# Late modulation in chunks that are loaded a step ahead and pinned on VectorE, head outputs loaded a group ahead, and half of the down weights in the activation buffers

## The chip, the cores and the metric

One core of one Trainium2 chip. The metric is the device time of one execution in microseconds (us); the lower the better. Matrix products run on TensorE (PE in the profile), elementwise work on VectorE (DVE) and ScalarE (ACT), and nearly all loads are issued in program order by SyncE (SP).

## The reference

One layer of a diffusion backbone: 512 latent tokens and 256 context tokens of width 2048. All matrix products are in fp32.

```python
mod = jax.nn.silu(c) @ w_mod[l] + b_mod[l]
sh1, sc1, ga1, sh2, sc2, ga2 = jnp.split(mod[:, None, :], N_MOD, axis=-1)
...
p_lat = modulate(rmsnorm(x, g_pre_mix[l]), sh1, sc1) @ w_in[l]
p_ctx = modulate(rmsnorm(ctx, g_pre_mix[l]), csh1, csc1) @ w_in[l]
m_lat, m_ctx = mlstm_group(p_lat, p_ctx, ...)      # 8 heads of 128
d_lat, d_ctx = diff_group(p_lat, p_ctx, cos, sin, lam, ...)   # 8 heads of 128
y_lat = jnp.concatenate([m_lat, d_lat], axis=-1).astype(x.dtype) @ w_out[l]
x = x + ga1 * rmsnorm(y_lat, g_post_mix[l])
h_lat = modulate(rmsnorm(x, g_pre_ffn[l]), sh2, sc2)
x = x + ga2 * rmsnorm(conv_ffn(h_lat, w_up[l], conv_ffn_w[l], conv_ffn_b[l], w_down[l]), g_post_ffn[l])
```

`sh1` and `sc1` are needed at once (`wmA`). The other four modulations (`ga1`, `sh2`, `sc2`, `ga2`, `wmB`, four times 2048 x 2048) are needed only after the heads: this is the late modulation.

## The kernel before

The kernel is one program in stages: start and first projections (0 to 240 us of the span), the head stage (240 to 1140), the first three groups of the output projection (1140 to 1262), its last group and the transition (1262 to 1380), the up projection (1380 to 2222), and the down projection with the end (2222 to 2733).

**Weights.** Every fp32 weight is split into two parts, `hi` (a cast on ScalarE) and `lo` (the rest, on VectorE), and each product is three matmuls: `whi` by `hi`, `whi` by `lo`, `wlo` by `hi` (`mm3`). A weight block arrives in raw tiles of 128 x 1024 (512 KB, pool `raw` with three buffers, shared with the late modulation), and `load_w` splits it into four `whi` and `wlo` tiles of 512 columns.

**Head stage.** `proj(m, with_ctx)` multiplies one weight block of 128 outputs with the latent tokens (`mm`, 512 columns) and, where asked, the context tokens (`cx`, 256 columns), in four groups g of four k tiles. For each head there are the projections diff_k, diff_v, mlstm_k and mlstm_v with context, and from head 5 on three latent projections (`lat_tile`). In this stage TensorE's instructions are pinned in program order, and `tick()` inserts pieces of the heads' attention between the matmuls: scores (`sc`), softmax (`mx` reduction on VectorE, `p` on ScalarE), transposes (`pt`), outputs. ScalarE's and VectorE's instructions are placed by the scheduler unless the code pins them.

**Late modulation.** It runs on VectorE. `modb_steps` is a generator: for each of 16 column blocks (q, cc) it loads raw tiles of `wmB` and adds them, scaled by the conditioning, into `macc` (L267 for the first, L269 for the others). A block is four steps of two raw tiles. `modb_cols` then sums over the partitions on TensorE (`modr`) and puts the columns into `mcol` (L283, L286). `step(limit)` runs one step: at the end of each projection and once at the start of heads 1 to 4 (limit 48, that is q = 0 to 2); the last 16 steps run in the down projection, at even `cc`.

**Output and down projection.** `nat_group` multiplies one group of four activation tiles (`mhi`, `mlo`) with four weight blocks and adds the products to `y` (L901). `get_mix(k)` brings a head output back, partly from DRAM (`mixr`). In the down projection odd `cc` take their weights through two wide tiles (`vhi`, `vlo`).

Of the kernel before, what the change touches and what calls it, by code (L numbers as in the profile page):

```python
# [6 lines left out]
F32 = mybir.dt.float32  # L7
F32R = mybir.dt.float32r
AF = mybir.ActivationFunctionType
ALU = mybir.AluOpType  # L10
# [4 lines left out]
P = 128  # L15
# [19 lines left out]
MIXG = [[0, 1, 2, 3], [8, 9, 10, 11], [4, 5, 12, 13], [6, 7, 14, 15]]  # L35
# [23 lines left out]
class Prog:  # L59
# [37 lines left out]
    def slot(self, name, dt=F32):  # L97
        return self.p_slot.tile([P, 512], dt, tag="slot", name=name)

    def load_w(self, src, n, act=False, wide=False):  # L100

        his, los = [], []
        if act:
            bh, bl = self.act("wact"), self.act("wact")
        if wide:
            for j in range(n // 1024):
                raw = self.p_raw.tile([P, 1024], F32, tag="raw", name="raw")
                self.nc.sync.dma_start(raw, src[:, j * 1024:(j + 1) * 1024])
                hi, lo = self.wide_w()
                self.split(hi, lo, raw)  # L110
                for q in range(2):
                    his.append(hi[:, q * 512:(q + 1) * 512])
                    los.append(lo[:, q * 512:(q + 1) * 512])
            n = 0
        for j in range(n // 512):
            if j % 2 == 0:
                w = min(1024, n - j * 512)
                raw = self.p_raw.tile([P, 1024], F32, tag="raw", name="raw")
                self.nc.sync.dma_start(raw[:, :w], src[:, j * 512:j * 512 + w])
            if act:  # L120
                hi, lo = bh[:, j, :], bl[:, j, :]
            else:
                hi = self.p_w.tile([P, 512], F32R, tag="whi", name="whi")
                lo = self.p_w.tile([P, 512], F32R, tag="wlo", name="wlo")
# [14 lines left out]
    def act(self, name):  # L139
        return self.p_act.tile([P, 4, 512], F32R, tag="act", name=name)  # L140

    def split(self, hi, lo, src):
        self.nc.scalar.copy(hi, src)  # L143
        self.nc.vector.tensor_tensor(lo, src, hi.bitcast(F32), ALU.subtract)  # L144

    def mm3(self, ps, whi, wlo, ahi, alo, start, stop, **k):
        mm = self.mm
# [103 lines left out]

    def modb_steps(self):

        nc, I = self.nc, self.I
        for q in range(4):
            for cc in range(4):
                acc = self.slot("macc")
                for kg in range(4):
                    for j in range(4):
                        if j % 2 == 0:  # L260
                            raw = self.p_raw.tile([P, 1024], F32, tag="raw", name="raw")
                            nc.sync.dma_start(raw, I["wmB"][q, cc, kg, :, j * 512:(j + 2) * 512])
                        kc = kg * 4 + j
                        c = self.c1[:, kc:kc + 1]
                        r = raw[:, j % 2 * 512:(j % 2 + 1) * 512]
                        if kc == 0:
                            nc.vector.tensor_scalar(acc, r, c, None, ALU.mult)  # L267
                        else:
                            nc.vector.scalar_tensor_tensor(acc, r, c, acc, ALU.mult, ALU.add)  # L269
                    if kg < 3:  # L270
                        yield
                self.defer(12, lambda q=q, cc=cc, acc=acc: self.modb_cols(q, cc, acc))
                yield

# [23 lines left out]
    def phase_in(self):  # L298
        nc, I = self.nc, self.I
        pc = self.p_c  # L300
        self.modc = pc.tile([P, KT, 4], F32, name="modc_sb")
        self.bA1 = pc.tile([P, KT], F32, name="bA1")
        self.c1 = pc.tile([P, KT], F32, name="c1")
        self.nlam = pc.tile([P, 1], F32, name="nlam")
        self.gg_d = self.dram.tile([2, D], F32, name="gg_d")
        self.mcol = pc.tile([P, 64], F32, name="mcol")

        lam = self.slot("lam")[:, :256]
        nc.sync.dma_start(lam, I["cols"][:, COLS["lam"][0]:])
# [12 lines left out]
        self.mix_d = self.dram.tile([KT, P, TL], F32, name="mix_d")  # L322
        self.acc_d = self.dram.tile([48, P, TL], F32, name="acc_d")
        self.acc = {}
        with self.tc.tile_pool(name="start", bufs=2) as self.p_st, \
                self.tc.tile_pool(name="mraw", bufs=4) as self.p_mr:
            self.startup()
            self.spill([b + h for h in (1, 2, 3) for b in (MQ, MO, DQ)])
            self.context()
            for base in (MQ, MO, DQ):  # L330
                self.lat_tile(base + 4)
            self.spill([b + 4 for b in (MQ, MO, DQ)])
        with self.tc.tile_pool(name="at1", bufs=1) as self.p_at1, \
                self.tc.tile_pool(name="cst", bufs=2) as self.p_cst, \
                self.tc.tile_pool(name="a3", bufs=14) as self.p_a3:
            self.attn_setup()
            self.pin = True
            self.gates_in(*self.proj(MG, True))
            self.queues[0].append(self.gates())
            for h in range(NH):  # L340
                if h >= 5:
                    for base in (MQ, MO, DQ):
                        self.lat_tile(base + h)
                elif h >= 1:
                    for base in (MQ, MO, DQ):
                        t = self.slot("accr")
                        nc.sync.dma_start(t, self.acc_d[base + h])
                        self.acc[base + h] = t
                hd = Head()
                if 0 < h < 5:  # L350
                    self.step(48)
                self.diff_q(hd, h)
                self.diff_k(hd, h, *self.proj(DK + h, True))
                self.diff_v(hd, h, *self.proj(DV + h, True))
                self.queues[1].append(self.diff_rest(hd, h))
                self.mlstm_qo(hd, h)
                self.mlstm_k(hd, h, *self.proj(MK + h, True))
# [95 lines left out]
    def proj(self, m, with_ctx):  # L453
        get = self.load_w(self.I["w1"][m], 2048)
# [4 lines left out]
        for g in range(4):  # L459
# [4 lines left out]
            if with_ctx:  # L464
                for kt in range(4 * g, 4 * g + 4):
                    c = self.chl[kt]
                    self.mm3(psc, *get(kt * P, P), c[:, :TC], c[:, TC:], kt == 0, kt == KT - 1)
                self.tick()
        self.step(48)
        return psl, psc  # L470


# [427 lines left out]
        else:  # L900
            nc.vector.tensor_tensor(y[tt][cc], ps, y[tt][cc], ALU.add)  # L901

    def nat_group(self, wsrc, acts, y, first, pool, tag, down=False):

        for cc in range(4):
            get = self.load_w(wsrc(cc), 2048, wide=down and cc % 2 == 1)
            if down and cc % 2 == 0:
                self.step(64)
            for tt in range(4):
                self.nat_unit(get, acts, tt, y, cc, first, pool, tag)  # L910

# [40 lines left out]
    def new_ss(self):  # L952
        return self.p_s.tile([P, 4], F32, tag="ss4", name="ss4", bufs=4)

    def mix_acts(self, g):
        hi, lo = self.act("mhi"), self.act("mlo")
        for j, k in enumerate(MIXG[g]):
            self.split(hi[:, j, :], lo[:, j, :], self.get_mix(k))
        return [hi[:, j, :] for j in range(4)], [lo[:, j, :] for j in range(4)]

    def phase_out_1(self):
        self.y = [[None] * 4 for _ in range(4)]
        nxt = self.mix_acts(0)
        for g in range(3):
            cur = nxt
            if g < 2:
                nxt = self.mix_acts(g + 1)
            self.nat_group(lambda cc: self.I["wo"][cc, g], cur, self.y, g == 0, self.ps_mm, "mm")

    def phase_out(self):  # L970
        nc, I = self.nc, self.I
# [383 lines left out]
```

## Time and profile before

| | |
|---|---|
| median of 3 runs | 2733.83 us (2731.48 to 2733.92) |
| profiled execution | 2734.44 us, span 2732.6 us |
| TensorE busy | 2643.5 us (97%) |
| VectorE busy | 1884.5 us (69%) |
| ScalarE busy | 1190.9 us (44%) |
| mean granted TensorE clock | 0.99 of full speed |
| DMA | 458.23 MB, mean 168 GB/s |

Times in rows are counted from the start of the span. A matmul's record is longer than the distance to the next one, since matmuls are pipelined. "Idle before" is the time that an engine stood still ahead of an instruction, with the instruction or DMA that ended it. Line numbers are those of the kernel before.

### The profile page before, as it was taken

The numbers are of one execution on the slowest core, as the hardware profiler recorded it, in microseconds if no ns is written. First come the engines' busy times: TensorE is split into PE (matmuls) and PEld (weight loads), VectorE is DVE, ScalarE is ACT, GpSimd is POOL, SyncE is SP. The second block draws the span as 40 slices with busy tenths as digits, with TensorE's granted clock in tenths as the row PEclk, the third lists the DMA queues.
The fourth block names the chain that finished last, engine by engine and source line by source line (L and its number), as shares of the span: only waits on it lengthen the run. The fifth ranks groups of instructions, "written<-read, shape, count | busy, mean of one in ns | idle before, by whom it ended". The sixth has DMA issues, their size and how long they took to land.

```text
span 2732.6 us, 43182 instructions
## 1 busy us (share of the span) xinstructions
PE 2643.5 (97%) x16916; PEld 2355.8 (86%) x16916; DVE 1884.5 (69%) x3252; ACT 1190.9 (44%) x2185; POOL 178.1 (7%) x233
## 2 busy tenths in 40 slices
PE   6999999999999999999699999999999999999998
PEld 3678798888888888877699999999999988888786
DVE  6585867766666666556887777778777775666556
ACT  4243344434434344424755555555555553222222
POOL 0000000000000000001111111111111100000000
PEclk9999999999999999999799999999999999999999
DMA  8765433433333434344487777777777764544434
GB/s 324 282 211 188 131 118 128 140 119 121 116 131 105 158 112 140 96 142 154 137 218 202 192 206 199 192 208 188 204 193 204 194 226 157 176 160 142 136 105 154
DMA packets 134749, 458.23 MB, mean 168 GB/s; under 512 B 15424, under 2 KB 15840, under 8 KB 130448
## 3 DMA queue, kind: packets, MB, share of 16 engines
q1 hardware_dynamic: 114704, 386.64, 43.0%
q0 software_dynamic: 19840, 68.83, 11.8%
q8 instruction: 133, 2.18, 0.3%
q14 instruction: 72, 0.59, 0.1%
HBM read 429.10 MB, written 26.30 MB: 167 GB/s over the span
## 4 chain that ended last, share of the span: by engine, by line
PE 49%; ACT 1%; DVE 1%; DMA 1%; issue 0%; DVEq 0%; POOLq 0%; POOL 0%; ACTq 0%
PE up L68 31%; PE nat L68 18%; ACT hf L1034 1%; DMA raw<-in_wu 0%; DMA raw<-in_wmB 0%; DVE S L1070 0%; DVE vlo L144 0%; ACT junk L927 0%; PE xt L71 0%; ACT vhi L143 0%; DVE wlo L144 0%; PE modr L68 0%; ACT S L1069 0%; DVE v L590 0%; DVE y L901 0%
## 5 line engine op out<-in xcount | busy, mean ns | idle before, releaser
L143 ACT CAST whi<-raw 128x512 fp32r<-128x512 f32 x492 | 302.1, 620 | 456.1 <-PE nat L68 139.9
L144 DVE TENSOR_TENSOR wlo<-raw,whi 128x512 fp32r<-128x512 f32 x492 | 336.0, 691 | 105.4 <-ACT whi L143 99.5
L68 PE MATMUL mm<-lhi,whi 128*128 128x512 f32 x912 | 370.7, 407 | 1.6 <-ACT whi L143 1.3
L68 PE MATMUL mm<-llo,whi 128*128 128x512 f32 x912 | 360.0, 395 | 0.8 <-DVE llo L249 0.8
L68 PE MATMUL mm<-lhi,wlo 128*128 128x512 f32 x912 | 358.8, 394 | 0.7 <-DVE wlo L144 0.7
L269 DVE SCALAR_TENSOR_TENSOR macc<-raw,c,macc 128x512 f32<-128x512 f32 x240 | 179.5, 748 | 128.3 <-DMA raw<-in_wmB 125.6
L68 PE MATMUL up<-S,whi 128*128 128x256 f32 x1408 | 258.2, 284 | 5.6 <-ACT S L1069 3.1
L68 PE MATMUL up<-S,vhi 128*128 128x256 f32 x1408 | 253.8, 281 | 1.6 <-ACT val L1168 1.0
L901 DVE TENSOR_TENSOR y<-nat,y 128x512 f32<-128x512 f32 x208 | 142.5, 687 | 129.7 <-PE nat L68 128.8
L68 PEld LDWEIGHTS up<-S,whi 128*128 128x128 f32 x1408 | 219.2, 192 | 6.2 <-ACT S L1069 3.3
L68 PEld LDWEIGHTS up<-S,vhi 128*128 128x128 f32 x1408 | 215.5, 188 | 2.0 <-ACT val L1168 1.2
L68 PEld LDWEIGHTS mm<-lhi,wlo 128*128 128x128 f32 x912 | 172.1, 189 | 41.3 <-issue 2.5
L68 PEld LDWEIGHTS mm<-lhi,whi 128*128 128x128 f32 x912 | 172.8, 190 | 34.6 <-ACT whi L143 2.7
L68 PE MATMUL up<-S,wlo 128*128 128x256 f32 x704 | 199.6, 284 | 2.3 <-DVE wlo L144 2.3
L68 PEld LDWEIGHTS mm<-llo,whi 128*128 128x128 f32 x912 | 173.0, 190 | 32.3 <-issue 3.7
L68 PE MATMUL cx<-chl,whi 128*128 128x256 f32 x1056 | 198.3, 286 | 2.0 <-ACT vt L629 2.0
L143 ACT CAST vhi<-raw 128x1024 fp32r<-128x1024 f32 x106 | 111.2, 1049 | 197.8 <-PE nat L68 154.2
L68 PE MATMUL up<-S,vlo 128*128 128x256 f32 x704 | 197.0, 280 | 0.0
L68 PE MATMUL up<-A,whi 128*128 128x256 f32 x1056 | 194.1, 284 | 0.0
L68 PE MATMUL up<-A,vhi 128*128 128x256 f32 x1056 | 193.0, 284 | 0.0
L68 PEld LDWEIGHTS cx<-chl,whi 128*128 128x128 f32 x1056 | 168.5, 191 | 9.7 <-ACT vt L629 2.8
L144 DVE TENSOR_TENSOR vlo<-raw,vhi 128x1024 fp32r<-128x1024 f32 x106 | 129.5, 1222 | 54.5 <-ACT vhi L143 54.2
(349 smaller groups left out, 5895.1 us busy)
## 6 DMA issues: line engine op xcount, KB each, us to landing
raw<-in_wu SPq DMA_DIRECT2D x132, 512.0 KB, 5.6
raw<-in_wmB SPq DMA_DIRECT2D x128, 512.0 KB, 4.1
raw<-in_w SPq DMA_DIRECT2D x105, 512.0 KB, 4.1
F<-in_wu SPq DMA_DIRECT2D x88, 512.0 KB, 5.4
F<-in_wu POOLq DMA_DIRECT2D x88, 512.0 KB, 7.8
raw<-in_wd SPq DMA_DIRECT2D x88, 512.0 KB, 4.4
mraw<-in_wmA SPq DMA_DIRECT2D x32, 1024.0 KB, 6.5
raw<-in_wo SPq DMA_DIRECT2D x32, 512.0 KB, 4.1
```

Source lines behind the costliest of these rows:

```text
L68: return self.pe(self.nc.tensor.matmul(*a, **k))
L143: self.nc.scalar.copy(hi, src)
L144: self.nc.vector.tensor_tensor(lo, src, hi.bitcast(F32), ALU.subtract)
L269: nc.vector.scalar_tensor_tensor(acc, r, c, acc, ALU.mult, ALU.add)
L901: nc.vector.tensor_tensor(y[tt][cc], ps, y[tt][cc], ALU.add)
L1034: nc.scalar.activation(h[:, js], pt[:, js], AF.Identity, bias=sh, scale=sc)
```

## The change

- The late modulation is cut into chunks of one raw tile. A step first computes the chunk that the step before has loaded (two `macc` operations, each pinned to its place in VectorE's program order), and then loads the next chunk, which stays in its raw buffer until the next step. A block has 9 steps, all of them 144.
- Steps are called inside `proj`: behind group 1, behind group 2 of projections with context, and behind group 3 (limit 108). The call at the end of a projection and that at the start of a head are gone. In the down projection a step is called at every `cc`, and the chunks of q = 3 use tiles of another pool (`F`).
- In the output projection the head outputs of the next group are fetched ahead of the current group, and their splits stand at `cc` = 2 of the current one, pinned on both engines.
- Weights with `act` are split 1024 wide into the buffers of the activation pool; in the down projection odd `cc` use this instead of `vhi` and `vlo`.

```diff
-    def load_w(self, src, n, act=False, wide=False):
+    def load_w(self, src, n, act=False):
...
         if act:
             bh, bl = self.act("wact"), self.act("wact")
-        if wide:
             for j in range(n // 1024):
                 raw = self.p_raw.tile([P, 1024], F32, tag="raw", name="raw")
                 self.nc.sync.dma_start(raw, src[:, j * 1024:(j + 1) * 1024])
-                hi, lo = self.wide_w()
-                self.split(hi, lo, raw)
...
+                js = slice(2 * j, 2 * j + 2)
+                self.split(bh[:, js, :], bl[:, js, :], raw.rearrange("p (a b) -> p a b", a=2))
...
-    def split(self, hi, lo, src):
-        self.nc.scalar.copy(hi, src)
-        self.nc.vector.tensor_tensor(lo, src, hi.bitcast(F32), ALU.subtract)
+    def split(self, hi, lo, src, keep=False):
+        a = self.nc.scalar.copy(hi, src)
+        b = self.nc.vector.tensor_tensor(lo, src, hi.bitcast(F32), ALU.subtract)
+        if keep:
+            self.tc.keep_in_program_order(a)
+            self.tc.keep_in_program_order(b)
...
         for q in range(4):
             for cc in range(4):
-                acc = self.slot("macc")
-                for kg in range(4):
-                    for j in range(4):
-                        if j % 2 == 0:
-                            raw = self.p_raw.tile([P, 1024], F32, tag="raw", name="raw")
-                            nc.sync.dma_start(raw, I["wmB"][q, cc, kg, :, j * 512:(j + 2) * 512])
-                        kc = kg * 4 + j
+                acc = None
+                for kg in range(8):
+                    raw = self.f_tile("raw") if q == 3 else self.p_raw.tile([P, 1024], F32, tag="raw", name="raw")
+                    nc.sync.dma_start(raw, I["wmB"][q, cc, kg // 2, :, kg % 2 * 1024:(kg % 2 + 1) * 1024])
+                    yield
+                    if acc is None:
+                        acc = self.slot("macc")
+                    for j in range(2):
+                        kc = kg * 2 + j
...
                         if kc == 0:
-                            nc.vector.tensor_scalar(acc, r, c, None, ALU.mult)
+                            ins = nc.vector.tensor_scalar(acc, r, c, None, ALU.mult)
                         else:
-                            nc.vector.scalar_tensor_tensor(acc, r, c, acc, ALU.mult, ALU.add)
-                    if kg < 3:
-                        yield
+                            ins = nc.vector.scalar_tensor_tensor(acc, r, c, acc, ALU.mult, ALU.add)
+                        self.tc.keep_in_program_order(ins)
...
-                if 0 < h < 5:
-                    self.step(48)
...
-        self.step(48)
+            if g == 3 or g == 1 or g == 2 and with_ctx:
+                self.step(108)
...
-            get = self.load_w(wsrc(cc), 2048, wide=down and cc % 2 == 1)
-            if down and cc % 2 == 0:
-                self.step(64)
+            get = self.load_w(wsrc(cc), 2048, act=down and cc % 2 == 1)
+            if down:
+                self.step(144)
+            if mid and cc == 2:
+                mid()
...
     def phase_out_1(self):
         self.y = [[None] * 4 for _ in range(4)]
-        nxt = self.mix_acts(0)
+        acts = [self.mix_acts(0)]
         for g in range(3):
-            cur = nxt
             if g < 2:
-                nxt = self.mix_acts(g + 1)
-            self.nat_group(lambda cc: self.I["wo"][cc, g], cur, self.y, g == 0, self.ps_mm, "mm")
+                for k in MIXG[g + 1]:
+                    self.get_mix(k)
+            self.nat_group(lambda cc: self.I["wo"][cc, g], acts[g], self.y, g == 0, self.ps_mm, "mm",
+                           mid=(lambda: acts.append(self.mix_acts(g + 1, True))) if g < 2 else None)
```

How the instructions stand now is shown at three places of the head stage. A name's number tells one buffer from another; `in_w1` are the projections' weights, `in_wmB` those of the late modulation.

First, VectorE ahead of an mlstm_v projection, in the mlstm_k projection. Before, `macc` of `raw_6739` and `raw_6743` stand among the output work of the mLSTM (`den`, `hn`); the weights `raw_6757` are loaded into the buffer that the second `macc` of `raw_6739` frees:

```order
L269 SCALAR_TENSOR_TENSOR macc_6290<-raw_6739,c1_95,macc_6290 128x512 x2
L724 SCALAR_TENSOR_TENSOR den_6474<-o_6469,fl_6475 128x2
L269 SCALAR_TENSOR_TENSOR macc_6290<-raw_6743,c1_95,macc_6290 128x512
L725 TENSOR_TENSOR den_6474<-o_6469,den_6474 128x2
L269 SCALAR_TENSOR_TENSOR macc_6290<-raw_6743,c1_95,macc_6290 128x512
L726 RECIPROCAL den_6474<-den_6474 128x2
```

Now, in the changed kernel, `macc` of `raw_6665` stands behind the softmax reduction (`mx`) of the score block that TensorE computes between groups 2 and 3:

```order
L809 TENSOR_REDUCE mx_6709<-sc_6710 128x1
L795 TENSOR_TENSOR ql_6874<-accr_6034,qa_6042 64x128
L810 TENSOR_SCALAR mx_6709<-mx_6709 128x1
L267 TENSOR_SCALAR macc_6722<-raw_6665,c1_95 128x512
L795 TENSOR_TENSOR ql_6874<-accr_6034,qa_6042 64x128
L269 SCALAR_TENSOR_TENSOR macc_6722<-raw_6665,c1_95,macc_6722 128x512
```

What moved: the last reading of the chunk whose buffer the next weights take stood behind results of TensorE that come 157 of its instructions ahead of these weights' first use; it stands now behind scores that come 35 instructions ahead of it.

Second, SP's loads at the same place. Before, two chunks of one step stand together ahead of the two weight tiles:

```order
L119 DMA raw_6539<-in_w1 128x1024
L119 DMA raw_6549<-in_w1 128x1024
L262 DMA raw_6739<-in_wmB 128x1024
L262 DMA raw_6743<-in_wmB 128x1024
L119 DMA raw_6757<-in_w1 128x1024
L119 DMA raw_6767<-in_w1 128x1024
```

Now three chunks, one for each step of the projection, stand ahead of them:

```order
L116 DMA raw_6555<-in_w1 128x1024
L116 DMA raw_6565<-in_w1 128x1024
L258 DMA raw_6665<-in_wmB 128x1024
L258 DMA raw_6725<-in_wmB 128x1024
L258 DMA raw_6770<-in_wmB 128x1024
L116 DMA raw_6782<-in_w1 128x1024
L116 DMA raw_6792<-in_w1 128x1024
```

What moved: `raw_6665`, `raw_6725` and `raw_6770` fill the three buffers; `raw_6782` waits for that of `raw_6665`, `raw_6792` for that of `raw_6725`.

Third, VectorE at the gates of the mLSTM (`g_...`, one long chain early in the head stage), where the weights `raw_2528` follow, which take the buffer of `raw_2448`. Before, the chunk of this place is read among the rotations of diff_q:

```order
L797 TENSOR_TENSOR ql_2724<-acc_362,qa_2311 64x128 x2
L267 TENSOR_SCALAR macc_2503<-raw_2504,c1_95 128x512
L269 SCALAR_TENSOR_TENSOR macc_2503<-raw_2504,c1_95,macc_2503 128x512
L521 MEMSET g_b_2354 40x768
L522 MEMSET g_m_2355 40x768
```

Now:

```order
L282 TENSOR_TENSOR mcol_98<-modr_2503,cols_87 128x4
L539 TENSOR_TENSOR g_dl_2385<-g_mp_2383,g_ml_2384 40x6
L548 TENSOR_TENSOR g_f_2352<-g_mp_2383,g_m_2355 40x768
L550 TENSOR_TENSOR g_l_2353<-g_i_2351,g_ml_2384 40x768
L555 TENSOR_TENSOR g_b_2354<-g_b_2354,g_m_2355 40x768
L551 TENSOR_SCALAR g_l_2353<-g_l_2353,g_dl_2385 8x128
L552 TENSOR_SCALAR g_l_2353<-g_l_2353,g_dl_2385 8x128
L267 TENSOR_SCALAR macc_2474<-raw_2448,c1_95 128x512
L285 SCALAR_TENSOR_TENSOR mcol_98<-mcol_98,cols_87 128x4
L745 STREAM_SHUFFLE rot_2517<-dk_2514 128x512
L269 SCALAR_TENSOR_TENSOR macc_2474<-raw_2448,c1_95,macc_2474 128x512
```

What moved: the chunk's first reading stood ahead of the gate chain's long operations, and stands now after nearly all of them.

## Rows read from the trace of the kernel before

**Rows 1.** The head stage's window: bounds, length, then each engine's busy us, clock, DMA share, GB/s.

```profile
240.00:1140.00 900.00, 880.92 (x5315) 777.76 (x5314) 605.90 (x1326) 374.30 (x810) 50.69 (x53) 0.99 0.38 126
```

**Rows 2.** What VectorE waited for, whole span: us in total, times, longest.

```profile
DVE macc L269 <- DMA raw<-in_wmB: 125.6, 72, 5.7
```

**Rows 3.** What TensorE waited for in the head stage, same columns.

```profile
PE sc L68 <- ACT p L814: 11.4, 5, 4.2
PE pt L71 <- DVE mx L812: 3.3, 1, 3.3
PE cx L68 <- ACT vt L629: 2.0, 2, 1.5
```

**Rows 4.** VectorE in order of time, 306 to 318: start, us, instruction, [idle before].

```profile
312.26 1.54 DVE L269 SCALAR_TENSOR_TENSOR macc<-raw,c,macc 128x512 f32<-128x512 f32 x2 [2.47 <-DMA raw<-in_wmB]
...
314.32 0.95 DVE L811 TENSOR_REDUCE mx<-sc 128x1 f32<-128x768 f32 x1
...
315.56 0.28 DVE L797 TENSOR_TENSOR ql<-acc,qa 64x128 fp32r<-64x128 f32 x1
```

**Rows 5.** TensorE in order of time, 308 to 320, and one stall near 503.

```profile
308.63 0.28 PE L68 MATMUL cx<-chl,wlo 128*128 128x256 f32 x1
308.75 0.40 PE L68 MATMUL mm<-lhi,whi 128*128 128x512 f32 x1
308.98 0.40 PE L68 MATMUL mm<-llo,whi 128*128 128x512 f32 x1
...
316.66 0.50 PE L68 MATMUL sc<-kb,qa 128*128 128x512 f32 x1 [2.88 <-ACT p L814]
...
503.33 0.50 PE L68 MATMUL sc<-kb,qa 128*128 128x512 f32 x1 [2.09 <-ACT p L814]
```

**Rows 6.** Four windows around stalls; the number before the DMA share is the clock.

```profile
310.00:330.00 20.00, 17.12 (x95) 14.60 (x94) 13.50 (x27) 6.84 (x14) 0.00 (x0) 0.91 0.40 129
690.00:710.00 20.00, 15.79 (x78) 13.40 (x77) 11.31 (x23) 6.39 (x12) 0.61 (x1) 0.83 0.34 115
2225.00:2235.00 10.00, 7.96 (x27) 5.86 (x26) 8.53 (x12) 6.71 (x11) 0.54 (x1) 0.83 0.86 285
2565.00:2575.00 10.00, 8.76 (x32) 7.08 (x33) 2.84 (x5) 0.00 (x0) 0.52 (x1) 0.83 0.59 188
```

**Rows 7.** TensorE in the output projection, 1170 to 1181.

```profile
1175.17 0.50 PE L68 MATMUL nat<-whi,mhi 128*128 128x512 f32 x1 [2.37 <-DVE y L901]
...
1178.64 0.50 PE L68 MATMUL nat<-whi,mhi 128*128 128x512 f32 x1 [0.45 <-ACT whi L143]
1179.60 0.50 PE L68 MATMUL nat<-wlo,mhi 128*128 128x512 f32 x1 [0.46 <-DVE wlo L144]
```

**Rows 8.** TensorE from up to down, 2225 to 2234.

```profile
2227.46 0.50 PE L68 MATMUL nat<-whi,ghi 128*128 128x512 f32 x1 [1.45 <-ACT whi L143]
2228.55 0.50 PE L68 MATMUL nat<-wlo,ghi 128*128 128x512 f32 x1 [0.58 <-DVE wlo L144]
```

**Rows 9.** TensorE ahead of the last group, 2564 to 2571.

```profile
2566.24 0.28 PE L71 MATMUL modr<-tabs,mcol 128*16 128x128 f32 x1 [2.08 <-DVE mcol L286]
```

**Rows 10.** One VectorE group of the head stage: xcount | busy us, mean ns | idle before.

```profile
L267 DVE TENSOR_SCALAR macc<-raw,c 128x512 f32<-128x512 f32 x11 | 5.3, 479 | 3.2 <-POOL row L664 3.1
```

**Rows 11.** Loads of the line of `in_w`, 240 to 1140.

```profile
DMA to landing us min/median/max: 3.6/4.0/5.9
```

**Rows 12.** All engines, 297 to 298: the late cast and the matmul behind it.

```profile
297.19 1.14 ACT L143 CAST whi<-raw 128x512 fp32r<-128x512 f32 x2 [3.21 <-DMA raw<-in_w]
...
297.86 0.50 PE L68 MATMUL mm<-lhi,whi 128*128 128x512 f32 x1 [1.04 <-ACT whi L143]
```

**Rows 13.** VectorE's gate chain, first and last, and TensorE's next projection.

```profile
272.05 0.94 DVE L516 SCALAR_TENSOR_TENSOR g_f<-g_f,g_l 40x768 f32<-40x768 f32 x1
...
277.95 0.47 PE L68 MATMUL mm<-lhi,whi 128*128 128x512 f32 x1
...
289.07 0.28 DVE L554 TENSOR_SCALAR g_l<-g_l,g_dl 8x128 f32<-8x128 f32 x1
```

More of the change, by code (lines that the diff above doesn't have):

```diff
@@ L108, in load_w @@
                 self.nc.sync.dma_start(raw, src[:, j * 1024:(j + 1) * 1024])
-                hi, lo = self.wide_w()
-                self.split(hi, lo, raw)
-                for q in range(2):
-                    his.append(hi[:, q * 512:(q + 1) * 512])
-                    los.append(lo[:, q * 512:(q + 1) * 512])
+                js = slice(2 * j, 2 * j + 2)
+                self.split(bh[:, js, :], bl[:, js, :], raw.rearrange("p (a b) -> p a b", a=2))
+            his, los = ([t[:, j, :] for j in range(n // 512)] for t in (bh, bl))
             n = 0
@@ L119, in load_w @@
                 self.nc.sync.dma_start(raw[:, :w], src[:, j * 512:j * 512 + w])
[L120 to L124, printed above, removed]
+            hi = self.p_w.tile([P, 512], F32R, tag="whi", name="whi")
+            lo = self.p_w.tile([P, 512], F32R, tag="wlo", name="wlo")
             self.split(hi, lo, raw[:, j % 2 * 512:(j % 2 + 1) * 512])
@@ L256, in modb_steps @@
             for cc in range(4):
-                acc = self.slot("macc")
-                for kg in range(4):
-                    for j in range(4):
-                        if j % 2 == 0:
-                            raw = self.p_raw.tile([P, 1024], F32, tag="raw", name="raw")
-                            nc.sync.dma_start(raw, I["wmB"][q, cc, kg, :, j * 512:(j + 2) * 512])
-                        kc = kg * 4 + j
+                acc = None
[7 more added lines that the diff above has]
+                        kc = kg * 2 + j
                         c = self.c1[:, kc:kc + 1]
-                        r = raw[:, j % 2 * 512:(j % 2 + 1) * 512]
+                        r = raw[:, j * 512:(j + 1) * 512]
                         if kc == 0:
-                            nc.vector.tensor_scalar(acc, r, c, None, ALU.mult)
+                            ins = nc.vector.tensor_scalar(acc, r, c, None, ALU.mult)
                         else:
-                            nc.vector.scalar_tensor_tensor(acc, r, c, acc, ALU.mult, ALU.add)
-                    if kg < 3:
-                        yield
+                            ins = nc.vector.scalar_tensor_tensor(acc, r, c, acc, ALU.mult, ALU.add)
+                        self.tc.keep_in_program_order(ins)
                 self.defer(12, lambda q=q, cc=cc, acc=acc: self.modb_cols(q, cc, acc))
@@ L901, in nat_unit, with nat_group @@
             nc.vector.tensor_tensor(y[tt][cc], ps, y[tt][cc], ALU.add)
-    def nat_group(self, wsrc, acts, y, first, pool, tag, down=False):
+    def nat_group(self, wsrc, acts, y, first, pool, tag, down=False, mid=None):
         for cc in range(4):
-            get = self.load_w(wsrc(cc), 2048, wide=down and cc % 2 == 1)
-            if down and cc % 2 == 0:
-                self.step(64)
+            get = self.load_w(wsrc(cc), 2048, act=down and cc % 2 == 1)
[3 more added lines that the diff above has]
+                mid()
             for tt in range(4):
@@ L953, in new_ss, with mix_acts @@
         return self.p_s.tile([P, 4], F32, tag="ss4", name="ss4", bufs=4)
-    def mix_acts(self, g):
+    def mix_acts(self, g, keep=False):
         hi, lo = self.act("mhi"), self.act("mlo")
         for j, k in enumerate(MIXG[g]):
-            self.split(hi[:, j, :], lo[:, j, :], self.get_mix(k))
+            self.split(hi[:, j, :], lo[:, j, :], self.get_mix(k), keep)
         return [hi[:, j, :] for j in range(4)], [lo[:, j, :] for j in range(4)]
```

## The prediction, made before the run

> **What bounds the kernel now.** I first read the busy times by stage. TensorE is the bound: 97% of the span (the table), and 880.92 of 900 us in the head stage [rows 1]. So the question is when TensorE stands still, and whether the change removes or adds such moments.
>
> Next I read who waits. VectorE waits 125.6 us for the raw tiles of `in_wmB`, the late modulation that the change moves [rows 2]. Most of that costs nothing, since VectorE is not the bound. It costs when TensorE needs something that stands behind the waiting `macc` in VectorE's queue. In the head stage TensorE waits 11.4 us for `p`, 3.3 for `mx` and 2.0 for `vt` [rows 3]. One instance, read through two engines: `macc` sat idle 2.47 us for its DMA until 312.26, the attention's `mx` reduction behind it began at 314.32 [rows 4], and the score matmul that needs the softmax came at 316.66, after 2.88 us of idle [rows 5]. All waits for `p`, all for `mx` and the longer `vt` wait (1.48) look like this: 11.4 + 3.3 + 1.5 = 16.2 us.
>
> Then the clock. After some stalls the granted clock drops: 0.91 in 310–330 and 0.83 in 690–710, 2225–2235 and 2565–2575 [rows 6]. The loss is (1 − clock) times the window: 1.7, 3.4, 1.7 and 1.7 us. Seven stalls are over 2 us: 2.88 and 2.09 [rows 5] and the longest for `p` (4.2) and for `mx` (3.3) [rows 3] in the head stage, then 2.37, 1.45 + 0.58 and 2.08 [rows 7 to 9]. Four were followed by the 1.2 GHz level. The loss per stall is 8.5 / 7 = 1.2 us.
>
> **What the change removes.** Each chunk is now loaded one step before VectorE computes on it, so the `macc` waits go. Head stage: 16.2 of idle and 1.7 + 3.4 of clock, 21.3. Out projection: the `mlo` splits that wait for spilled head outputs no longer stand ahead of the `y` additions. TensorE's waits there, 2.37, 0.45 and 0.46 [rows 7], go: 3.3. Up to down: the first down step now only issues a load, which removes 1.45 + 0.58 [rows 8] and the 1.7 of clock: 3.7. The transposed column `modr` at 2566.24 waits 2.08 for `mcol` [rows 9]; a 512-wide `wlo` now stands there instead of a 1024-wide `vlo`, so I take 1.5 (0.9 without, 3.8 with its clock dip). Sum 29.8.
>
> At nothing I cost: the wider casts of the out group and of nat_last and the even/odd exchange of down buffers (same elements; TensorE has tens of us of matmuls per weight block there to hide them), and the pinned `mid` splits (about 2 us of cover per output unit; if it failed, some 0.5 us each).
>
> **What it adds: late weight loads.** There are three raw buffers for weights and chunks, and one chunk is now held between two steps. A step is called behind group g = 1, 2 and 3 of a projection. As built, the first weight tile of projection n+1 usually takes the buffer of the chunk that is computed at g = 2 of projection n. That computation is pinned behind the attention's operations of that place, which wait for TensorE. Only the matmuls of g = 3 are left as cover.
>
> Worked through for `raw_6782` of the first two places shown in the order: the last score matmul ends; VectorE then does reduce, `ql`, `mx`, `macc`, `ql`, `macc`. From the reduce's start to the end of the second `ql` is 1.5 us [rows 4]; the two `macc` are 0.48 and 0.75 [rows 4, 10]; overlapped, 2.6. SP issues the load, which lands in 4.0 us (3.6 to 5.9) [rows 11]. TensorE starts 0.67 after the cast starts (297.19 to 297.86 [rows 12]). From the start of the last score matmul to its end beyond its pitch is another 0.16 (0.28 long at a pitch of 0.12 [rows 5]). In all 7.4. TensorE's work in that time is 12 matmuls of 512 columns at 0.23, 12 of 256 at 0.12 [rows 5], and ten small ones, which I also take at 0.12: 5.2 us. So it waits about 2.3.
>
> All weight loads of the head stage, by the same sum over their own rows of the order:
> - A, eleven loads with this pattern (first weight tiles of projections whose predecessor has scores between its groups 2 and 3): VectorE 33.5, landing and cast 11 × 4.83, TensorE's cover 55.2. Late by 33.5 + 53.1 − 55.2 = 31.4.
> - B, `raw_2528`, the first load after the gates: its chunk stands behind the whole gate computation, because its first `macc` now comes in VectorE's order after `mcol` and the gate operations (the third place shown). In the trace of before these run from 272.05 to 289.35, while TensorE starts the projection in question at 277.95 [rows 13]. Without the two `wlo` and one `ql` between them (1.7) and with two `macc` (1.2) VectorE is through at 288.8; landing at 292.8, TensorE at 293.5: late by 15.5. If the scans were through sooner, the ten operations from `mcol` on alone would leave 10.
> - C, `raw_4624` and `raw_5363`: only four small matmuls (0.4) between the `modr` columns on which VectorE waits and the weights' use; VectorE 1.3: 1.3 + 4.83 − 0.4 = 5.7 each, 11.4.
> - D, nine loads with 6.5 to 12 us of cover: 0 to 9.6 together. Most come out at half a us or less, so I take 3.
> Sum 61.3. In the kernel before, every weight load has 16 us or more of matmuls behind its release. The load that landed latest cost 1.04 us [rows 12].
>
> Each late start has two riders. The third matmul waits for `wlo`: nothing visible to 0.58 us ([rows 8], the second row); 14 starts, 3 to 8 us, I take 5. And the clock: fourteen stalls over 2 us at 1.2 give 17 (0 if none dips; 24 if each loses 1.7). A rule bears on this. The Trainium skill, "TensorE: Matmul & The Clock Gate", section "HAM oscillation — how this bites in real kernels", says that a loop which waits for DMA between groups of matmuls falls back to the cold clock at every such wait. By that the term would be 24 and the time 7 us longer. The trace agrees only in part (four of seven stalls, [rows 6]), so I stay at 17.
>
> Added: 61.3 + 5 + 17 = 83.3. Net 83.3 − 29.8 = +53.5. The profiled execution took 2734.4 us (span 2732.6); its result is 2787.9. The median shown is 0.6 lower, so I say **2787**.
>
> **Rivals.**
> Weights in time (faster): the scheduler's buffers or SP's order let those loads go before the chunk is computed, so that only the removed waits count: 2733.8 − 29.8 = 2704. For it: at 0.38 mean DMA share in the head stage there is bandwidth to spare [rows 1], and VectorE has a third of its time free. Against it: SP takes its DMAs in order, and each waits for its buffer. The sign turns where the added terms fall under 29.8; B and C with their riders alone are 27 + 5. So C's, B's and most of A's lateness would have to be hidden together. The Trainium skill's "Trainium Kernel Development and Optimization", "Best Practices", asks for double buffering to overlap DMA with compute; by that the load-ahead gives this time. The rows agree for the chunks, not for the weights, which lose the buffer that the held chunk keeps.
>
> Half the size (still slower): landing at the minimum of 3.6 (14 × 0.4 = 5.6 less), B at 10 (5.5 less), D nothing (3), `wlo` 3 (2), no clock dips (17): 33 less, 2754. For it: three of seven stalls had no dip. Against: the median landing is 4.0, and the loads now start under load of others.
>
> No effect within 0.2% (about 5.5 us, what a measurement of this kernel can tell from no change): gains and losses would have to cancel.
>
> **How the numbers follow.** My sum 0.58, own range 2770 to 2808: A moves by 4.4 with landings 0.4 shorter or longer, D from 0 to 9.6, the clock by 7 upward. Half size 0.24 (2740 to 2770). Weights in time 0.11. Same 0.03. Above 2808 (landings near 5, all dips) 0.04. The range 2748 to 2810 leaves out the faster and the equal case and the edges of the others, 2 in 10. Faster 0.11, same 0.03, slower 0.86.
>
> **What would show it.** Right: TensorE's waits in the head stage for `whi` from `mm`, about a dozen of 2 to 3.5 us, two near 6 and one of 10 to 16 us shortly after 278; ScalarE's `whi` waiting for DMA `raw<-in_w` just before each; `macc` no longer waiting for `in_wmB`; a granted clock in the head stage under 0.99; out-projection and down stages 3 and 4 us shorter. Wrong: the `whi` casts of first tiles sitting done before TensorE arrives, and the head stage under 900 us.

## The result and the profile after

The changed kernel takes 2822.97 us (median, 2822.48 to 2823.99), the kernel before 2733.88 beside it: a ratio of 1.0326, 95% interval 1.031 to 1.0343. The span of the profiled execution is 2820.7 us, 88.1 more than before. The direction was forecast, the size was not: 2787 stood against it, and 2810 as the upper end.

Where the time went is seen in busy times by stage, cut at the same instructions in both kernels (window, length, then busy us of TensorE, its weight loads, VectorE, ScalarE, GpSimd, then clock, DMA share, GB/s). The kernel before:

```profile
240.00:1106.00 866.00, 846.92 (x5124) 748.50 (x5122) 590.13 (x1293) 356.19 (x770) 49.69 (x52) 0.99 0.39 128
1106.00:1348.00 242.00, 221.87 (x1077) 184.50 (x1078) 150.63 (x295) 123.48 (x285) 18.69 (x29) 0.95 0.40 129
1348.00:2224.00 876.00, 866.48 (x7273) 865.17 (x7272) 684.48 (x911) 487.91 (x769) 97.64 (x128) 1.00 0.75 199
2224.00:2733.00 509.00, 494.15 (x2151) 402.32 (x2149) 298.75 (x429) 136.11 (x203) 3.24 (x6) 0.99 0.47 154
```

The changed kernel, same view:

```profile
240.00:1208.00 968.00, 882.72 (x5128) 769.95 (x5128) 594.34 (x1291) 358.26 (x767) 48.61 (x52) 0.95 0.35 115
1208.00:1448.00 240.00, 220.75 (x1076) 183.94 (x1076) 151.47 (x290) 123.94 (x281) 18.73 (x29) 0.96 0.41 131
1448.00:2324.00 876.00, 867.82 (x7272) 866.33 (x7271) 683.59 (x910) 487.72 (x770) 97.65 (x128) 0.99 0.75 199
2324.00:2821.00 497.00, 484.23 (x2153) 400.45 (x2151) 299.46 (x423) 134.82 (x196) 3.24 (x6) 0.99 0.48 158
```

The head stage is 102 us longer, the output projection and the transition 2 shorter, the up projection the same, the down part 12 shorter: 88 together. In the head stage TensorE does the same matmuls (5124 and 5128 records) in 35.8 us more of busy time, which is the lower clock (0.95 against 0.99), and stands still 85.3 us (968 − 882.7) instead of 19.1.

What it stood still for, in the waits of TensorE over the span (us in total, times, longest), those that [rows 3] do not have (in the head stage of the kernel before `whi` cost 1.0 us and `wlo` 0.7):

```profile
PE mm L68 <- ACT whi L137: 76.2, 20, 16.1
...
PE mm L68 <- DVE wlo L138: 4.0, 9, 1.1
PE o L68 <- POOL row L662: 3.6, 2, 1.9
```

19 of the 20 waits for `whi`, 76.0 us, lie in the head stage. The worked example of the prediction, in the order of time over all engines (start, us, engine, instruction, [idle before]):

```profile
764.74 0.28 PE L68 MATMUL sc<-kb,ql 128*128 128x256 f32 x1
...
765.27 0.95 DVE L809 TENSOR_REDUCE mx<-sc 128x1 f32<-128x768 f32 x1
...
767.48 0.75 DVE L269 SCALAR_TENSOR_TENSOR macc<-raw,c,macc 128x512 f32<-128x512 f32 x1
...
768.26 4.67 SPq L116 DMA_DIRECT2D raw<-in_w  x2
...
772.12 1.14 ACT L137 CAST whi<-raw 128x512 fp32r<-128x512 f32 x2 [1.65 <-DMA raw<-in_w]
...
772.79 0.79 PE L68 MATMUL mm<-lhi,whi 128*128 128x512 f32 x1 [2.14 <-ACT whi L137]
```

The reduction starts at 765.27, the second `macc` ends at 768.23, SyncE issues the weights at 768.26, the cast starts 3.86 us later and TensorE 0.67 after that: it waited 2.14 where 2.3 was worked out. That the two agree so well is in part luck: behind the last score matmul (764.74, 0.12 to the next start) the chain took 7.9 us where 7.4 was worked out, and TensorE had work for 5.8 us of them where 5.2 was; both were some half a us short, and the difference came out right. The load behind the gates, same view:

```profile
287.19 0.49 DVE L267 TENSOR_SCALAR macc<-raw,c 128x512 f32<-128x512 f32 x1
...
288.30 0.73 DVE L269 SCALAR_TENSOR_TENSOR macc<-raw,c,macc 128x512 f32<-128x512 f32 x1
...
289.06 2.85 SPq L116 DMA_DIRECT2D raw<-in_w  x2
...
292.25 1.69 ACT L774 CAST kb<-dk 64x768 fp32r<-64x768 f32 x2 [3.16 <-DVE dk L748]
...
293.96 1.14 ACT L137 CAST whi<-raw 128x512 fp32r<-128x512 f32 x2
294.63 0.79 PE L68 MATMUL mm<-lhi,whi 128*128 128x512 f32 x1 [16.14 <-ACT whi L137]
```

VectorE was through at 289.03 (288.8 in the prediction), TensorE waited 16.14 (15.5). The last step was not only the landing: the first tile landed at 293.17, and its cast stood until 293.96 behind ScalarE's `kb`, which waited for VectorE. What the change set out to remove did go: what VectorE stood still for ahead of `macc` in the head stage (us, times) is

```profile
  DMA raw<-in_wmB: 6.8, 6
  POOL row L662: 4.0, 1
```

where the waits for the DMA were 67.2 us in 41 before.

What a late start costs beyond its wait is seen in TensorE's own rows behind one of them:

```profile
422.08 0.50 PE L68 MATMUL mm<-lhi,whi 128*128 128x512 f32 x1 [3.26 <-ACT whi L137]
...
424.09 0.63 PE L68 MATMUL mm<-lhi,whi 128*128 128x512 f32 x1
424.52 0.63 PE L68 MATMUL mm<-llo,whi 128*128 128x512 f32 x1
```

Two microseconds after the stall the matmuls stand 0.43 us apart instead of 0.23 (the 1.2 GHz level), until 427.3.

### The profile page after: what moved, and what is told of

Read it like the earlier page. It is cut to its first block, busy times and chain, and to the rows that moved or that the text cites. A ratio compares the mean times of both kernels' runs of the same rounds, so it can differ in the third digit from the quotient of the medians.

```text
span 2820.7 us, 43046 instructions
## 1 busy us (share of the span) xinstructions
PE 2671.1 (95%) x16916; PEld 2376.5 (84%) x16916; DVE 1890.1 (67%) x3238; ACT 1191.9 (42%) x2171; POOL 177.1 (6%) x233
## 3 DMA queue, kind: packets, MB, share of 16 engines
q0 software_dynamic: 19840, 68.83, 11.4%
## 4 chain that ended last, share of the span: by engine, by line
PE 47%; DVE 1%; ACT 1%; DMA 1%; issue 0%; POOL 0%; DVEq 0%; POOLq 0%; ACTq 0%
PE up L68 30%; PE nat L68 17%; ACT hf L1035 1%; DMA raw<-in_wu 0%; DMA raw<-in_wd 0%; DVE S L1071 0%; DVE wlo L138 0%; PE xt L71 0%; DVE A L1071 0%; DVE vlo L138 0%; PE modr L68 0%; ACT S L1070 0%; DVE xn L993 0%; ACT vhi L137 0%; ACT whi L137 0%
## 5 line engine op out<-in xcount | busy, mean ns | idle before, releaser
L68 PE MATMUL mm<-lhi,whi 128*128 128x512 f32 x912 | 382.0, 420 | 76.2 <-ACT whi L137 76.2
L68 PE MATMUL mm<-lhi,wlo 128*128 128x512 f32 x912 | 370.2, 407 | 4.0 <-DVE wlo L138 4.0
L68 PE MATMUL mm<-llo,whi 128*128 128x512 f32 x912 | 369.3, 405 | 0.0
L68 PE MATMUL nat<-wact,ghi 128*128 128x512 f32 x640 | 197.2, 389 | 0.0
L68 PEld LDWEIGHTS up<-A,whi 128*128 128x128 f32 x1056 | 164.0, 191 | 0.0
```

The source lines that it names most:

```text
L68: return self.pe(self.nc.tensor.matmul(*a, **k))
```

## The experiments

Three theories stood at the start. **H**: weights wait for the raw buffer that a held chunk keeps, and the chunk's reading is pinned so late that too little cover is left. **P**: the pinned `macc` delay the attention's VectorE work by themselves. **S**: three steps in a projection crowd the queues. All ratios are to the kernel before, timed on the same chip; there it took 2734.99 us beside own_a12, early, unpin and dnbuf, 2740.09 beside own_pool, ctrl12, early_gate and pad, and 2736.07 beside the last three, so a few us against a window given in us can be the chip's.

**Chunks in a buffer of their own** (own_a12):

```diff
+        self.p_ck = self.p_raw
...
-                    raw = self.f_tile("raw") if q == 3 else self.p_raw.tile([P, 1024], F32, tag="raw", name="raw")
+                    raw = self.f_tile("raw") if q == 3 else self.p_ck.tile([P, 1024], F32, tag="raw", name="raw")
...
-                self.tc.tile_pool(name="a3", bufs=14) as self.p_a3:
+                self.tc.tile_pool(name="a3", bufs=12) as self.p_a3, \
+                self.tc.tile_pool(name="ck", bufs=1) as self.p_ck:
```

> The changed kernel, but in the head stage the chunks of the late modulation get a buffer of their own (one tile of 128 x 1024), so the three raw buffers serve weights alone; room for it comes from two of the fourteen attention buffers. Pins and places of the steps stay. Theory H (weights wait for the buffer that a held chunk keeps): no weight load is late any more, TensorE's waits for whi in the head stage fall from 76 us to under 8 and the clock loss there from about 42 us to under 10; the head stage is about 20 us shorter than in the kernel before, the whole about 2700 us (2692 to 2715). Rival P (the pinned macc delay the attention's own VectorE work, whatever the buffers): the pins are untouched, so the time stays over 2780. Rival S (three steps and more loads in a projection crowd the DMA queue): same as P, over 2780.

2727.82 us, ratio 0.9976 (0.9962 to 0.999). H holds against P and S: pins and steps are the same, and 95 us are gone. No wait for `whi` is left in the head stage, and TensorE's busy time there is 848.8. But the 2692 to 2715 were missed: the head stage ends 3 us later than before, not 20 earlier. `macc` waits for its DMA again (first line), and TensorE for results that follow VectorE (`p`, `kw`):

```profile
  DMA raw<-in_wmB: 64.8, 38
...
PE sc L68 <- ACT p L814: 7.7, 8, 3.6
PE vtp L71 <- DVE kw L675: 6.6, 4, 3.0
```

What the whole gained lies behind the head stage: the down part is 10 us shorter than before.

**Steps ahead of the group instead of behind it** (early):

```diff
         for g in range(4):
+            if g == 3 or g == 1 or g == 2 and with_ctx:
+                self.step(108)
...
-            if g == 3 or g == 1 or g == 2 and with_ctx:
-                self.step(108)
```

> The changed kernel with the step called ahead of the matmuls of groups 1, 2 and 3 instead of behind them; buffers, pins and number of steps stay. Theory H, in the form that cover decides: the chunk whose buffer the next weights take is read one group earlier, so 5 us or more of matmuls are added to the cover of each load. Nearly all of the lateness goes; what stays is the load behind the gates (5 to 10 us instead of 16) and the two behind modr (1 to 4 us each instead of 5 and 9.5). TensorE's waits for whi in the head stage 10 to 20 us, whole 2712 to 2740. Rivals P and S (pins, more steps): nothing of either changes, over 2780.

2745.65 us, 1.0042 (1.0026 to 1.0058), a little over the window; the waits are those of H (the head stage, to 1130):

```profile
PE mm L68 <- ACT whi L137: 21.7, 3, 15.9
```

One group more of cover takes 54 of the 76 us away. The load behind the gates stays, and is 15.9, not 5 to 10.

**No pins on macc** (unpin):

```diff
-                        self.tc.keep_in_program_order(ins)
```

> The changed kernel without the pins on macc; the scheduler may move these operations on VectorE. As built it puts them ahead of the attention's work, except behind modr twice. Theory H with P as its half (the held buffer hurts only because the pinned reading comes so late): late loads 6 us each at two places and little else, waits for whi 10 to 20 us, whole 2705 to 2740. If the held buffer alone did it, the time would stay over 2790; if the pins alone did it, about 2700.

2754.82 us, 1.0076 (1.0056 to 1.0095): 15 us over the window. Waits for `whi` are 18.0 us in three: 4.8 and 9.3 behind `modr`, as forecast, and 3.9 near 301. But `macc` waits 57.7 us for its DMA, and TensorE 18 us for `p`, `mx` and `kw`, which were not forecast. So held buffer and late reading are both needed for the 76 us, and without pins the old waits are back.

**Only the new weight buffers** (dnbuf; the kernel before with the new `load_w` and this):

```diff
-            get = self.load_w(wsrc(cc), 2048, wide=down and cc % 2 == 1)
+            get = self.load_w(wsrc(cc), 2048, act=down and cc % 2 == 1)
```

> The kernel before with only the new weight buffers: odd cc of the down projection (and the act loads of the output projection and of the last group) are split 1024 wide into buffers of the activation pool instead of vhi and vlo. The down part gained 12 us with the change, 7 more than the waits that were counted. Theory R (a matmul that reads vhi or vlo takes longer than one that reads the activation buffers: records of 393 to 397 ns against 389): 960 such matmuls at 6.5 ns, about 6 us; 2725 to 2730. Rival W (the gain came from the waits alone, which this edit leaves): 2732 to 2736.

2737.21 us, 1.0008 (0.9996 to 1.0019): no gain, W by the time, but the rows say R with a loss beside it. Matmul records of odd `cc` fell to 389 ns (from one start to the next 227 ns instead of 234, medians in the traces), which for 960 matmuls is some 6.5 us, and in the down part seven waits for `y` came up, 6.5 us together. One of them, and what held VectorE:

```profile
2299.78 0.49 DVE L261 TENSOR_SCALAR macc<-raw,c 128x512 f32<-128x512 f32 x1 [4.06 <-DMA raw<-in_wmB]
2300.19 0.68 DVE L895 TENSOR_TENSOR y<-nat,y 128x512 f32<-128x512 f32 x1
...
2300.93 0.50 PE L68 MATMUL nat<-whi,ghi 128*128 128x512 f32 x1 [1.41 <-DVE y L895]
```

The addition to `y` stands behind a `macc` that waits for its load. So alone the new buffers gain nothing, and in the changed kernel, where no wait for `y` is left in the down part, they do; the chunks without the new buffers were not run.

**Chunk loads from GpSimd** (own_pool; own_a12 with `nc.gpsimd.dma_start` for the chunks of q = 0 to 2):

> The run own_a12 (chunks in a buffer of their own, two attention buffers fewer), with one edit more: in the head stage the chunk loads are issued by GpSimd instead of SyncE. In own_a12 macc still waited 64.8 us for its DMA in the head stage, as in the kernel before, and TensorE 20 us for p, kw and others. Theory Q (SyncE issues in order, so a chunk's load stands behind a weight load that waits for its own buffer, and lands late although its buffer is free): from another queue the chunk lands in time, macc waits fall under 15 us, TensorE's waits in the head stage from 20 to under 10, the whole 2705 to 2720. Rival D (with one buffer there is no time to load it between two steps, whatever the queue): macc waits stay over 50 us, the time at 2722 to 2732.

2759.82 us, 1.0075 (1.0061 to 1.0089). Q falls: `macc` waits 98.8 us instead of 64.8, TensorE 20.3 for `p` and 15.7 for `kw`. With one buffer there is too little time between two steps, as D had it. It came out some 28 us above D's window too. Nearly all of this lies in the head stage, which ends at 1143 instead of 1109, and the chunks did come later there: a load was issued 0.3 us (median) behind the `macc` that freed the buffer, where SyncE took 0.03, and then took longer to land (own_pool, then own_a12):

```profile
DMA to landing us min/median/max: 3.9/4.3/7.0
...
DMA to landing us min/median/max: 3.5/3.8/6.7
```

That GpSimd held the loads up with other work explains little: the longest such delay was 3.0 us.

**The control for two attention buffers fewer** (ctrl12; the kernel before with `bufs=12`):

> The kernel before with twelve attention buffers instead of fourteen, nothing else: the control for own_a12. If the two buffers cost what own_a12 did not win (its head stage ended 3 us later than that of the kernel before, with 6.6 us of a new wait for kw), the head stage is 10 to 20 us longer here and the whole 2744 to 2755. If they cost nothing, 2730 to 2738 and no wait for kw.

2739.16 us, 0.9998 (0.9989 to 1.0008): they cost nothing that can be measured. (The wait for `kw` was 0.5 us.)

**No step beside the gates** (early_gate):

```diff
-            if g == 3 or g == 1 or g == 2 and with_ctx:
+            if (g == 3 or g == 1 or g == 2 and with_ctx) and m != DK:
```

> The run early (steps ahead of groups 1 to 3), with one edit more: no step in the first diff_k projection, the one beside the gate computation. In early TensorE still waited 15.9 us for the first weights behind the gates. Theory H: the chunk that held this load's buffer was pinned among the gates; without it that wait goes, nothing else changes: waits for whi in the head stage from 21.7 to 3 to 9 us (steps move on by one place and meet modr at two others), the whole 2723 to 2733. Rival G (the gate computation itself keeps the weights or the cast late): the wait of 10 us or more stays, 2740 to 2750.

2738.50 us, 0.9998 (0.9989 to 1.0007), 5 us above the window. The 15.9 us wait is gone (waits for `whi` 9.2 us, the longest 2.9), so H holds there and G falls. But TensorE now waits 10.5 us for `p`. One such place:

```profile
702.11 1.14 ACT L137 CAST whi<-raw 128x512 fp32r<-128x512 f32 x2 [3.96 <-DMA raw<-in_w]
...
702.77 0.69 DVE L138 TENSOR_TENSOR wlo<-raw,whi 128x512 fp32r<-128x512 f32 x1 [3.03 <-ACT whi L137]
...
704.04 0.95 DVE L809 TENSOR_REDUCE mx<-sc 128x1 f32<-128x768 f32 x1
...
706.79 0.80 PE L68 MATMUL sc<-kb,qa 128*128 128x512 f32 x1 [3.56 <-ACT p L812]
```

This is the chain of [rows 4, 5] with `wlo` in the place of `macc`: now the weights' split waits at VectorE's head, for a cast that waits for its load, and the softmax stands behind it. From this came theory **B**: with three buffers for both streams one of the two is always late, and whichever waits at VectorE's head holds the attention back.

**The FFN coefficients' tile widened, so that vhi and vlo move** (pad):

```diff
-            self.cff = self.p_x.tile([P, 88 * 4], F32, name="cff", bufs=1)
+            self.cff = self.p_x.tile([P, 512], F32, name="cff", bufs=1)[:, :88 * 4]
```

> The kernel before with the FFN coefficients' tile widened from 352 to 512 columns, which moves the tiles behind it in the same pool, vhi and vlo among them, by 640 bytes; no work changes. In the down projection a matmul that reads vhi or vlo has records of 393 to 397 ns, one that reads whi or the activation buffers 387 to 389. Theory A (it is where the tile lies): with the start of the tiles moved to a multiple of 2 KB the records fall to 389 and the down projection gets some 6 us shorter, 2726 to 2731. Rival T (it is that the tile is wider or in another pool, or what else touches it): records stay at 393 to 397, 2732 to 2737.

2747.45 us, 1.0026 (1.0015 to 1.0037). A falls as it was put: the records did not get shorter. The kernel before, the changed kernel and pad, in the listing of TensorE's line for the down projection (count, then min/median/max ns):

```profile
L68 PE MATMUL nat<-vhi,ghi x319: 393/396/399, 2240.3 to 2677.8; 128*128 128x512 f32 x160
```

```profile
L68 PE MATMUL nat<-wact,ghi x640: 387/389/486, 2337.4 to 2766.6; 128*128 128x512 f32 x160
```

```profile
L68 PE MATMUL nat<-vhi,ghi x320: 392/397/400, 2249.1 to 2688.3; 128*128 128x512 f32 x160
```

T's time was missed as well: pad takes 7 us more than the kernel before on the same chip. They lie in the up projection, which also reads `vhi` and `vlo`. In the window that is cut as above, the kernel before has 876.00 us with 866.48 of TensorE, ctrl12, on pad's chip, 876.00 with 867.63, and pad:

```profile
1352.00:2235.00 883.00, 874.45 (x7269) 872.99 (x7268) 684.55 (x911) 486.94 (x768) 97.75 (x128) 0.99 0.75 197
```

There the matmuls with `vhi` or `vlo` start 1.4 to 1.8 ns further apart than before (means in the traces), those with `whi` or `wlo` between 0.7 less and 0.9 more; for 3690 matmuls that is some 6 us. So where tiles lie does bear on these times, of these tiles or of others that the edit moved; how is open.

**Two buffers of their own** (own2_a11: own_a12 with `a3` at 11 and `ck` at 2):

> The changed kernel with two buffers of their own for the chunks in the head stage, so the three raw buffers serve weights alone; room comes from three of the fourteen attention buffers (two were shown to cost nothing). Theory B (buffers decide: whichever instruction waits at VectorE's head for a late DMA, macc or wlo, holds back the softmax behind it; with one own buffer it was macc again): with two, chunks and weights both land in time, macc waits in the head stage under 15 us, no waits for whi, TensorE's waits there under 8 us, the head stage 15 us or more shorter than before, the whole 0.985 to 0.990 of the kernel before. Rival P2 (the pinned macc themselves hold back the softmax): waits for p and kw stay at 15 us or more, ratio 0.995 to 1.000. Rival A11 (eleven attention buffers are too few): waits of the attention's splits and copies for PE appear, ratio over 1.000.

2701.53 us, ratio 0.9877 (0.9862 to 0.9892): faster than both kernels. In the head stage `macc` waits 7.9 us for its DMA, TensorE 5.0 us in all, and its busy time has little clock loss in it (one dip, 0.77 in 295 to 310, around a wait of 2.9 us for `wlo`):

```profile
  DMA raw<-in_wmB: 7.9, 6
...
240.00:1089.00 849.00, 843.80 (x5129) 748.23 (x5129) 593.23 (x1291) 358.11 (x768) 49.38 (x52) 1.00 0.39 130
```

The head stage is 20 us shorter than in own_a12, with one buffer more for the chunks and one less for the attention. B holds; P2 and A11 fall.

**The same without pins** (own2_unpin):

> The run own2_a11 without the pins on macc. Theory B: the pins matter only through the buffer that they keep, so nothing is gained or lost against own2_a11 (within 5 us). Rival P2: TensorE's waits for p and kw fall and it is 10 us or more faster than own2_a11.

2719.21 us, 0.9944 (0.9924 to 0.9963): 18 us slower. Neither reading was right: the pins help. 13 of the 18 us lie in the head stage. Without the pins `macc` waits 29.8 us there for its DMA (24 times), TensorE 5.8 for `p` again. So an early `macc` meets a load that is still under way; pinned, it mostly comes when the load has landed.

**The changed kernel without the step beside the gates** (after_gate; the edit of early_gate on the changed kernel):

> The changed kernel without a step in the first diff_k projection, the one beside the gates. It takes away the longest late load (16 us) and moves the steps on by one projection; some 13 loads stay late, 40 to 50 us together by the sum of VectorE work, landing and cover. What a late start costs in clock: theory C (nearly every stall of 2 us or more is followed by half speed for 3.4 us or more, about 2 us each): loss of clock in the head stage 25 to 36 us, whole 2770 to 2800. Rival C0 (much of the 42 us of clock lost in the changed kernel came with the 16 us stall): clock loss there under 20 us, whole 2745 to 2770.

2799.20 us, 1.0235 (1.022 to 1.025), at the upper end of C's window. Waits for `whi` are 58.4 us in 15, more than the 40 to 50 in some 13 that were expected. They and the busy time of its head stage:

```profile
PE mm L68 <- ACT whi L137: 58.4, 15, 9.1
...
240.00:1182.00 942.00, 875.21 (x5129) 766.77 (x5128) 592.88 (x1291) 355.31 (x769) 49.75 (x52) 0.95 0.35 118
```

Against own2_a11, with the same 5129 matmuls, that is 31.4 us of clock, 2.1 per wait, though the longest stall is gone. C0 falls.

## Why the prediction was right or wrong

**Right: the mechanism and its places.** Late first weight tiles behind a pinned reading, the pattern, the load behind the gates, the two behind `modr`. The head stage's 19 waits, put in order beside the prediction's groups of loads: A 35.4 us in eleven (31.4 forecast), B 16.1 (15.5), C 14.5 (11.4), D 9.9 in five (3). The `wlo` rider came to 4.0 (5). The worked example agreed better than it should have: besides what is said above, its own terms for TensorE's work (12 × 0.23, 12 × 0.12, 10 × 0.12) make 5.4, not 5.2. And that every weight load before has 16 us or more of matmuls behind its release does not hold for the load of [rows 12], which was issued at 291.30, 6.6 us ahead of its matmul.

**Wrong in size: the clock.** The step is "fourteen stalls over 2 us at 1.2 give 17". The head stage's busy time is 38.9 us above that of own2_a11: 19 waits at 2.0. The rate of 1.2 was taken from seven stalls of the kernel before, of which three kept their clock; here 15 of the 19 late starts have a stretch at 1.2 GHz at or behind them, in after_gate (2.1 per wait) 13 of 15. Why stalls of the same length kept the clock more often in the kernel before is not shown. The other sum that the prediction weighed, 24, was nearer. The Trainium skill ("TensorE: Matmul & The Clock Gate", "HAM oscillation — how this bites in real kernels") tells of a loop that starts cold after every one of its DMA waits; the waits there are longer than most of these, and 15 of 19 is nearer to it than four of seven. This term is 22 of the 35 us by which the result lay off.

**Wrong in size: the late loads.** 76.0 instead of 61.3. D went over its upper bound of 9.6, and one of C was 9.55 instead of 5.7: the sums added VectorE's work behind the release, but not what VectorE itself waits for there. Before the first `macc` of that load of C VectorE stood still 4.0 us for GpSimd's `row`; [rows 10] show such a wait of 3.1 in the kernel before. In three of D's five places VectorE waited 2.1 to 2.2 us for ScalarE's `hn`, which waited for a DMA (`mix_d`); in the other two the load took 5.1 and 5.7 us from issue to landing, where 4.0 was put in. A's 4.0 more was not traced to single places. Two waits that the sum did not have, 3.6 for `row` and 1.6 for `p`, came on top. Either of the two terms alone would have left the time inside the range of 2748 to 2810; both together did not.

**The gains.** Forecast 29.8. In the head stage the old waits did go (`macc` 6.8 instead of 67.2), as far as can be told beside the new ones; own2_a11, without the new ones, shows them: its head stage ends at 1089, 17 us earlier than before (21.3 forecast), and the whole gains 33.3 us of span. The out part and the transition gave 2 (3.3). The down part gave 12 (5.2): 2.1 of idle and 9.9 of busy time, of which 3.4 are the two clock dips of [rows 6] and about 6 a term that was not in the sum, 960 matmuls that read the activation buffers at 389 ns instead of `vhi` and `vlo` at 394 to 396.

**The balance.** Forecast was +53.5, found 88.1 of span: clock 22 more, late loads 15, other waits 4, the down part 7 less, and about 1 over from the smaller items and rounding.

**The rivals.** The result lies in the case above 2808, to which the prediction gave 0.04 for "landings near 5, all dips": the dips nearly all came, the landings did not (median 3.9 us). Of "Half the size" nothing came: the load behind the gates waited 16.1 us, D 9.9, and the clock fell. "Weights in time", 2704, is what own2_a11 reaches with 2701.5: the price of that case was right in total (its parts less so, see the gains), its condition was not met by the change. What met it is the number of buffers (one of its own 0.9976, two 0.9877) together with the pins (0.9944 without); loads from another queue did not help (own_pool).

## What to carry to other kernels

A tile that is loaded a step ahead occupies its buffer for that whole step: count the buffers of the pool again, and find who takes the released one next. When two streams share a pool and both are read by one in-order engine, removing the wait of one can return as a wait of the other; give the prefetched stream its own buffers, two of them, and look for the room among pools whose depth costs nothing that can be measured (here two of fourteen attention buffers). Where a buffer is released by an engine that runs in order, add to its work what it waits for itself (here 4.0 us in one place). And price a repeated stall of a few microseconds by its wait plus what the clock loses around it (here 2 us each), not by the average of a few single stalls.

## What the runs showed of the hardware that was not expected

Matmuls with the same shapes and the same clock took 393 to 399 ns in the records when they read `vhi` and `vlo`, and mostly 387 to 389 from `whi` or the activation buffers, all through the down projection; from start to start it is 234 against 227 ns (medians). Moving those tiles by 640 bytes left them at 392 to 400, and the width of the split is the same in dnbuf, where the records are 389. In the up projection the same move made the matmuls with these tiles some 1.6 ns slower each. What makes the difference stays open; it was not tried to put these tiles farther away in memory.
